# A hybrid attention layer on one core: how far ahead weight loads are issued, and where the summing steps of the output weights stand

## The chip, the cores and the metric

The kernel runs on one core of a Trainium2 chip. Its engines are TensorE (PE, matmuls), VectorE (DVE), ScalarE (ACT), GpSimd (POOL) and SyncE (SP, which here only issues DMA transfers). The metric is device time in microseconds; the profile gives the starts and durations of the instructions on each engine.

## The reference

One layer on 512 tokens and 16 meta tokens (528 positions) of width 2048, in fp32:

```python
hn = rmsnorm(h, pre_norm_g)
qa, ka, va, ga, qb, kb, vb, gb = split(hn @ w_in)     # widths 1024, 256, 256, then five of 1024
# mixer A: 8 query heads of 128 on 2 key/value heads, RMS-normed q and k, rotary
ya = softmax(rope(norm(qa)) @ rope(norm(ka)).T / sqrt(128)) @ va * silu(ga)
# mixer B: 8 heads, each with two score matrices on 64 of the 128 columns
a  = softmax(q1 @ k1.T / 8 + bias) - lam * softmax(q2 @ k2.T / 8 + bias)
yb = rmsnorm(a @ vb, sub_g) * (1 - lambda_init) * silu(gb)
y  = concat(ya, yb) @ w_out
out = h + rmsnorm(y, post_norm_g)                     # without the meta tokens
```

## The kernel before

**Precision and chunks.** Every fp32 operand of a matmul is split into a high and a low part, and a product is three matmuls (high by high, low by high, high by low). The weights of a projection come in chunks of 512 KB: a load into a tile `st` (L149, on SP's queue), the high part `wh` by ACT (L156), the low part `wl` by DVE (L157), then 24 or 48 matmuls for the eight 128-row pieces in it (`pd`). The pool `wp` has three buffers each of `st`, `wh` and `wl`. `todo` lists the chunks to come, `chunks` those whose load and split are written into the program; `fetch` keeps two beyond the one in hand. In this kernel a chunk's load and its two splits are thus always written together.

**Stage B (to about 490 us).** For each of 8 heads the projections of gate, value, key and query (two chunks each, `dense_T`) run while the attention of an earlier head is woven between their matmuls: scores `sc` (L61, psum), added bias and row maximum (`mx`, `p`, DVE L521), exponentials (`p`, `sm`, ACT L529), the reciprocal (DVE L531), the scaling of the first p by GpSimd (L534), the difference of the two p by DVE (L536), 32-by-32 transposes (`pt`, DVE), a turn through DRAM (`turn` out, L455; four pieces of `pl` and one of `pt` back, L461 and L462, all on SP's queue), the split of that into `ph` (ACT), `pl` (DVE) and `pm`, and p times v (`pv`). The query of the next head is split by L337 (`q`, four pieces, ACT) and L340 (`l`, four pieces, DVE).

**Sums of output weights.** The output product of the last stage uses 32 blocks `ws` of 512 KB in DRAM that are sums of blocks of `w_out` with each other. Each sum is one step: a transfer on SP's queue (L141: a copy `ws<-ws` of an earlier sum, or a load `ws<-in_w_o_dram`), and an adding DMA on GpSimd's queue (L809). `weigh(n)` takes n steps; of each it first issues the add that belongs to the step before, so that one load is always waiting for its add. It is called at three places of a head: two steps ahead of the gate, two after it, and one after the values.

**Stages A and C.** From about 490 to 745 us the 8 heads of mixer A follow (normalization and rotary of q and k: `qn`, `kn`; transposed queries split into `qh` and `qlA`; scores, `mxA`, p, turn and `pv` as above), between the projections of A and the 8 gates (`gt`, with a table load on ACT before and after the gate's own function). Then come the output products `po`, which load chunks of `ws` and `w_out` into `st` by the same `fetch`, and the end at 908 us.

**What sets the order.** PE's order and that of the loads written by `load()` (L141) are the program's. Tasks of attention are put between dense matmuls by `Lanes`: a virtual clock counts the matmuls' time, and a task sleeps for a lag from the table `LAG` (in us of that clock; `pB` and `pA` are the lags from the regrouping of p to p times v in mixers B and A). The order on ACT, DVE, GpSimd and of the other DMAs on SP is chosen when the program is built, by a scheduler that goes by priorities (the splits of weights have a raised one) and by its own idea of when operands are ready. Each engine and each queue works strictly in the order so set.

Of the kernel before, what the change touches and what calls it, by code (L numbers as in the profile page):

```python
# [10 lines left out]
F32 = mybir.dt.float32  # L11
# [3 lines left out]
ALU = mybir.AluOpType  # L15
AX = mybir.AxisListType

P = 128
# [11 lines left out]


LAG = dict(vals=3.5, bank=2.8, bankA=1.5, bankB=2.5, turnA=1.5, turnB=1.5, pvA=5.0, pvB=6.0, scB=3.0,
           pB=22.0, ss=6.0, qA=2.35, scA=5.1, pA=16.0, rope=10.2, head=3.85, fin=1.35, qn=1.4, norm=4.0, valsA=(10.0, 7.0),
           steps=(3.0, 2.5, 2.0, 2.0), stepsK=(2.5, 2.0, 1.5))

AHEAD = -60
# [70 lines left out]
def kernel(ctx: ExitStack, tc: tile.TileContext, xT, xn, xm, w_s, w_t, w_q, w_o,  # L107
                             gpre, gq, gk, lams, gsub, gpost, ident_d, cos_d, sin_d, dist_d, out):
    nc = tc.nc
# [6 lines left out]
    wp = ctx.enter_context(tc.tile_pool(name="wp", bufs=3))  # L116
# [22 lines left out]
    def load(out, in_):  # L139

        tc.keep_in_program_order(nc.sync.dma_start(out=out, in_=in_))  # L141


    def wload(src, n=1024, dma=nc.sync.dma_start, parts=1):
        st = wp.tile([P, 1024], F32, name="st", tag="st")
        ws = None
        for i in range(parts):
            c = slice(i * n // parts, (i + 1) * n // parts)
            dma(out=st[:, c], in_=src if parts == 1 else src[:, c])  # L149
            ws = wsplit(st, c, ws)  # L150
        return ws
# [43 lines left out]
    KEYS = [(0, HALF), (HALF, NT)]  # L195
    REAL = [(NM, NT)]
# [4 lines left out]
        mm(ps, wl, xh[k][:, n0:n1], start=False, stop=(k == KT - 1))  # L201


    todo, chunks = [], []

    def fetch(ahead=2):
        while todo and len(chunks) <= ahead:
            src = todo.pop(0)
            chunks.append(src() if callable(src) else wload(src))
        return chunks.pop(0)  # L210

    def dense_T(segs, pss=None, half=None):

        pss = pss or [pd.tile([P, 512], F32, name="pd", tag="pd") for _ in segs]
        for k0 in range(0, KT, 8):
            wh, wl = fetch()
            for k in range(k0, k0 + 8):
                c = slice((k - k0) * P, (k - k0 + 1) * P)
                for (n0, n1), ps in zip(segs, pss):
                    three(ps[:, :n1 - n0], wh[:, c], wl[:, c], k, n0, n1)  # L220
                    lanes.poll()
                if half and k == 8:
                    half()
        return pss
# [38 lines left out]
    for t in (TT, 0, 1, 2, 3):  # L263
        rows = P if t < TT else NM
        src = xn[t * P:(t + 1) * P, :] if t < TT else xm
        for j in range(2 if t < 2 else 4):

            tag, w = ("pl", "pt")[j % 2], 1024
# [73 lines left out]
    def keys_B(pss, after=nullcontext):  # L342
        kf = ap.tile([P, NT], F32, name="kf", tag="tT")
        halves(pss, kf)
        s1 = ap.tile([P, NT], F32R, name="s1", tag="s1")
        s2 = ap.tile([P, NT], F32R, name="s2", tag="s2")
        with after():
            hi(s1[L], kf[L])
            hi(s2[U], kf[U])
            lo(s1[U], kf[L], s1[L])  # L350
            lo(s2[L], kf[U], s2[U])
        return s1, s2
# [43 lines left out]
    def values(pss, lag=LAG["vals"]):  # L396

        vf = ap.tile([P, NT], F32, name="vf", tag="tT")
        halves(pss, vf)
        vh = ap.tile([P, TT, P], F32R, name="vh", tag="vh")  # L400
        vl = ap.tile([P, TT, P], F32R, name="vl", tag="vl")
        vm = ap.tile([96, P], F32R, name="vm", tag="vm")
        nc.vector.memset(vm.bitcast(F32), 0.0)

        def turn():
            yield from whole()
            tr = ptr.tile([P, 512], F32, name="tr", tag="tr")
            for c in range(TT):
                transpose(tr[:, c * P:(c + 1) * P], vf[:, NM + c * P:NM + (c + 1) * P], ident)
            tv = tr.rearrange("p (c d) -> p c d", d=P)  # L410
            hi(vh, tv)
            lo(vl, tv, vh)
            yield LAG["bank"]
            yield from whole()
            tr = ptr.tile([P, 512], F32, name="tr", tag="tr")
            transpose(tr[:NM, :P], vf[:, 0:NM], ident)
            hi(vm[0:NM], tr[0:NM, :P])
            hi(vm[64:64 + NM], tr[0:NM, :P])
            lo(vm[32:32 + NM], tr[0:NM, :P], vm[0:NM])

        return (vh, vl, vm), lanes.spawn(turn(), lag)

    def gate(pss, name):
        g = gp.tile([P, SEQ], F32, name=name, tag="g", bufs=4)
        nc.vector.tensor_tensor(out=g, in0=pss[0], in1=rB[:, NM:], op=ALU.mult)
        nc.scalar.activation(g, g, AF.Silu)
        return g
# [369 lines left out]
    steps, adds = [], []  # L797
# [4 lines left out]
        steps += [(S[2][i], S[1][i], block(p, 0, 1, i)) for i in range(4)]  # L802
        steps += [(S[3][i], block(p, 0, 0, i), block(p, 1, 0, i)) for i in range(4)]

    def weigh(n=1):
        for _ in range(n):
            if adds:
                dst, src = adds.pop(0)
                nc.gpsimd.dma_start(out=dst, in_=src, accum_op=ALU.add)  # L809
            if steps:  # L810
                dst, src, add = steps.pop(0)
                load(dst, src)
                adds.append((dst, add))

    def otile(name, n, dt=F32R):
        return xtile(name, n, dt)[:, NM:NT]
# [48 lines left out]
    def finish_head(h):  # L865
        lanes.finish(heads[h])
        lanes.finish(over[h])

    for h in range(NH):
        heads[h] = lanes.spawn(attention_B(h, qs, ks, *v), LAG["head"], heads[h - 1])  # L870
        if h == 2:
            tables()
        if h > 0:
            weigh(2)
            gB[h] = gate(dense_T(REAL), f"gB{h}")
        if h + 1 < NH:
            if h:
                weigh(2)
            pss = dense_T(KEYS)
            if h:  # L880
                finish_head(h - 1)
            v = values(pss)
            if h:
                weigh()
            ks = keys_B(dense_T(KEYS))
            qs = queries_B(h + 1, dense_T(REAL))
    weigh()
    def start_heads(grp, qn, q_task, k, v):
# [76 lines left out]
    def product(ops, pss, more=False, beside=None, done=None, ahead=2):  # L965


        def step(u, i, ws):
            for j in range(2):
                bh, bl = ops(i, j, u)  # L970
                c = slice(j * 512, (j + 1) * 512)
                wh, wl = ws[j] if isinstance(ws, list) else [w[:, c] for w in ws]
                mm(pss[u], bh, wh, start=(i + j == 0 and not more), stop=False,
                   skip_group_check=more)
                mm(pss[u], bl, wh, start=False, stop=False, skip_group_check=more)
                mm(pss[u], bh, wl, start=False, stop=(i + j == 4), skip_group_check=more)
                lanes.poll()

        for i in range(1 if done else 4):
            ws = fetch(ahead)  # L980
            for u in range(2):
                step(u, i, ws)
            if beside:
                beside(i)
        if done:
            last = [fetch(len(todo)) for _ in range(3)]
            for u in range(2):
                for i in range(3):
                    step(u, 1 + i, last[i])
                done(u, pss[u])  # L990
        return pss
# [259 lines left out]
```

## Time and profile before

| | us |
|---|---|
| median of 3 runs | 913.62 |
| lowest and highest | 912.55, 913.66 |
| the profiled execution, its own time | 910.12 |
| its span, from the first to the last instruction | 908.3 |
| mean granted TensorE clock | 0.984 of full speed |

The tables of the prediction come from this one execution. A row of a timeline has the start in us, the duration in us, the engine, the line of the kernel, the operation, output and inputs by their names, shapes, how many such instructions stand together (x4), and in brackets the engine's idle time ahead of the first of them with what ended it. `SPq` is the queue of SyncE; a row of it shows the issue of a DMA, not its transfer. In a row of the transfers' table stand what is moved, the count, the size of one and the median time from issue to landing. A row of a table by windows has the stretch, its length, then the busy time and the count of instructions of PE, PE's weight loads, DVE, ACT and POOL, then the granted clock, the share of the 16 DMA engines and GB/s.

### The profile page before, as it was taken

To read this page: it belongs to the slowest core of one execution; us is meant where nothing else is said; L and a number is where in the kernel's file an instruction comes from. 1 tells how busy PE (TensorE), PEld (TensorE's weight loads), DVE (VectorE), ACT (ScalarE), POOL (GpSimd) and SP (SyncE) were. 2 spreads that over 40 slices of the span, in tenths; PEclk is the share of its full clock that TensorE was granted. 3 is DMA by queue.
4 is the path that set the end of the run, shared out by engine and by line. 5 is a ranking of instruction groups with operands and counts; after the bars stand their busy time and mean duration, and the time that the engine had idled before them with its cause. 6 is when DMAs were issued, how large, how long until landed. Compare 5 with 4: busy or idle time off the path is not lost. (4 is left out here: it accounts for less than half of the span.)

```text
span 908.3 us, 14068 instructions
## 1 busy us (share of the span) xinstructions
PE 877.6 (97%) x5130; PEld 777.5 (86%) x5130; DVE 633.0 (70%) x1137; ACT 498.6 (55%) x844; POOL 126.7 (14%) x168
## 2 busy tenths in 40 slices
PE   9999999799989999999999999989989899999996
PEld 8999898798979989899898888978878788888884
DVE  6677785576846868575783485788664775876886
ACT  6564664445646456473754444566674565665561
POOL 0101112011111211111020021341211120000010
PEclk9999999899999999999999999999999899999998
DMA  9748759678595785968353334456566568889883
GB/s 342 260 152 238 196 180 264 169 227 218 158 287 131 225 255 157 291 171 254 115 180 93 105 92 153 136 156 180 169 167 187 179 197 306 289 284 305 294 257 150
DMA packets 80677, 185.49 MB, mean 204 GB/s; under 512 B 15136, under 2 KB 38560, under 8 KB 80224
## 3 DMA queue, kind: packets, MB, share of 16 engines
q1 hardware_dynamic: 75856, 167.81, 56.4%
q0 software_dynamic: 4608, 16.78, 10.7%
q8 instruction: 40, 0.66, 0.3%
q14 instruction: 29, 0.24, 0.1%
q10 hardware_dynamic: 144, 0.01, 0.0%
HBM read 158.34 MB, written 59.77 MB: 240 GB/s over the span
## 5 line engine op out<-in xcount | busy, mean ns | idle before, releaser
L61 PE MATMUL pd<-xh,wh 128*128 128x264 f32 (+1 forms) x992 | 328.6, 331 | 0.1
L61 PE MATMUL pd<-xl,wh 128*128 128x264 f32 (+1 forms) x992 | 325.7, 328 | 0.1
L61 PE MATMUL pd<-xh,wl 128*128 128x264 f32 (+1 forms) x992 | 324.6, 327 | 0.0
L156 ACT ACTIVATE wh<-st 128x1024 fp32r<-128x1024 f32 (+2 forms) x159 | 165.4, 1041 | 187.0 <-PE pd L61 95.4
L157 DVE TENSOR_TENSOR wl<-st,wh 128x1024 fp32r<-128x1024 f32 (+2 forms) x159 | 191.1, 1202 | 92.9 <-ACT wh L156 91.3
L61 PEld LDWEIGHTS pd<-xh,wl 128*128 128x128 f32 x992 | 188.3, 190 | 16.3 <-DVE wl L157 0.2
L61 PEld LDWEIGHTS pd<-xh,wh 128*128 128x128 f32 x992 | 188.8, 190 | 12.6 <-ACT wh L156 0.4
L61 PEld LDWEIGHTS pd<-xl,wh 128*128 128x128 f32 x992 | 188.9, 190 | 11.1 <-DVE xl L192 0.4
L529 ACT ACTIVATE p<-p,mx 128x528 f32<-128x528 f32 x64 | 47.1, 736 | 57.0 <-DVE mx L521 56.8
L448 DVE STREAM_TRANSPOSE pt<-p 128x512 f32<-128x512 f32 x64 | 45.2, 706 | 10.7 <-POOL p L629 9.9
L534 POOL TENSOR_SCALAR p<-p,sm 128x528 f32<-128x528 f32 x32 | 23.0, 718 | 208.9 <-DVE sm L531 208.7
L61 PE MATMUL pd<-wh,xh 128*128 128x512 f32 x128 | 50.4, 394 | 0.0
L61 PE MATMUL pd<-wh,xl 128*128 128x512 f32 x128 | 49.9, 390 | 0.0
L61 PE MATMUL pd<-wl,xh 128*128 128x512 f32 x128 | 49.9, 390 | 0.0
L521 DVE CUSTOM_DVE_ANT_0 p<-sc,dist 128x528 f32<-128x528 f32 x64 | 44.0, 688 | 6.5 <-PE sc L61 6.0
L627 ACT ACTIVATE p<-p,mxA 128x528 f32<-128x528 f32 x32 | 23.5, 735 | 40.1 <-DVE mxA L624 40.0
L340 DVE TENSOR_TENSOR pl<-pl,ph 128x1024 fp32r<-128x1024 f32 x32 | 40.4, 1261 | 5.7 <-ACT ph L337 5.2
L61 PE MATMUL sc<-s,q 128*128 128x264 f32 x128 | 35.6, 297 | 8.9 <-DVE mx L521 6.6
L809 POOL DMA_DIRECT2D ws<-in_w_o_dram x32 | 26.6, 841 | 121.9 <-DMA ws<-ws 54.2
L629 POOL TENSOR_SCALAR p<-p,smA 128x528 f32<-128x528 f32 x32 | 25.8, 806 | 122.1 <-DVE smA L628 118.4
L61 PE MATMUL pv<-ph,vh 128*128 128x256 f32 x128 | 37.2, 291 | 2.9 <-DMA st<-in_w_t_dram 2.9
L536 DVE SCALAR_TENSOR_TENSOR p<-p,c 128x528 f32<-128x528 f32 x32 | 24.5, 766 | 21.4 <-POOL p L534 21.2
(223 smaller groups left out, 1578.8 us busy)
## 6 DMA issues: line engine op xcount, KB each, us to landing
st<-in_w_t_dram SPq DMA_DIRECT2D x82, 512.0 KB, 5.5
turn<-pt SPq DMA_DIRECT2D x32, 544.0 KB, 3.0
ws<-in_w_o_dram POOLq DMA_DIRECT2D x32, 512.0 KB, 9.3
pl<-turn SPq DMA_DIRECT2D x128, 128.0 KB, 3.7
st<-ws SPq DMA_DIRECT2D x32, 512.0 KB, 4.5
st<-in_w_o_dram SPq DMA_DIRECT2D x22, 512.0 KB, 4.7
ws<-in_w_o_dram SPq DMA_DIRECT2D x16, 512.0 KB, 7.5
ws<-ws SPq DMA_DIRECT2D x16, 512.0 KB, 6.3
```

Of the source, the lines that this page charges most:

```text
L61: self._add(self.nc.tensor.matmul(out, lhsT, rhs, start=start, stop=stop, **kw), us)
L156: splits.append((nc.scalar.activation(wh[:, c], st[:, c], AF.Copy), nc.vector.tensor_tensor(out=wl[:, c], in0=st[:, c], in1=wh[:, c].bitca ...
L157: nc.vector.tensor_tensor(out=wl[:, c], in0=st[:, c], in1=wh[:, c].bitcast(F32), op=ALU.subtract)))
L340: nc.vector.tensor_tensor(out=dst, in0=src, in1=h.bitcast(F32), op=ALU.subtract)
L448: nc.vector.transpose(pt[:, :1024].rearrange("p (m c t q) -> p c m t q", m=4, c=TT, t=2)[:, :, :, j], p[:, NM:].rearrange("p (c m q) -> p ...
L521: maxima.append(nc.vector.tensor_tensor_reduce(out=two(p), in0=sc[:, :, :HALF], in1=two(dist[:, w0:w0 + NT]), scale=-0.125 / slope(h), sca ...
L529: nc.scalar.activation(p2[m], p2[m], AF.Exp, scale=-1.0, bias=mx[:, m:m + 1], accum_out=sm[:, m:m + 1])
L534: nc.gpsimd.tensor_scalar(out=p2[0], in0=p2[0], scalar1=sm[:, 0:1], scalar2=1.0, op0=ALU.mult, op1=ALU.mult)
L536: nc.vector.scalar_tensor_tensor(out=p2[0], in0=p2[1], scalar=c2, in1=p2[0], op0=ALU.mult, op1=ALU.add)
L627: nc.scalar.activation(p, p, AF.Exp, scale=-1.0, bias=mx, accum_out=sm)
L629: nc.gpsimd.tensor_scalar(out=p, in0=p, scalar1=sm, scalar2=1.0, op0=ALU.mult, op1=ALU.mult)
L809: nc.gpsimd.dma_start(out=dst, in_=src, accum_op=ALU.add)
```

## The change

The change adds no instruction and takes none away; it moves them. It has four parts.

1. A load and its splits are written apart. A new `bring` issues the load of a chunk; the splits are written when `fetch` moves the chunk from `landing` to `chunks`. `fetch` keeps two loads issued beyond the chunks it has split. Tiles are as many as before.
2. `weigh` takes one step, not n, and is called at five places of a head: ahead of the gate, in the middle of it, after it, after the values' projection and after the keys'. An add follows two loads behind, not one.
3. The lag `pA` goes from 16 to 13.5.
4. The last product, which fetches all that is left, counts `landing` too.

```diff
-           pB=22.0, ss=6.0, qA=2.35, scA=5.1, pA=16.0, rope=10.2, ...
+           pB=22.0, ss=6.0, qA=2.35, scA=5.1, pA=13.5, rope=10.2, ...
...
-    todo, chunks = [], []
+    todo, chunks, landing = [], [], []
+
+    def bring():
+        src = todo.pop(0)
+        if not callable(src):
+            st = wp.tile([P, 1024], F32, name="st", tag="st")
+            nc.sync.dma_start(out=st, in_=src)
+            src = lambda: wsplit(st)
+        landing.append(src)
 
     def fetch(ahead=2):
-        while todo and len(chunks) <= ahead:
-            src = todo.pop(0)
-            chunks.append(src() if callable(src) else wload(src))
+
+        while (todo or landing) and len(chunks) <= ahead:
+            if not landing:
+                bring()
+            chunks.append(landing.pop(0)())
+        while todo and len(landing) < 2 and not callable(todo[0]):
+            bring()
         return chunks.pop(0)
...
-    def weigh(n=1):
-        for _ in range(n):
-            if adds:
-                dst, src = adds.pop(0)
-                nc.gpsimd.dma_start(out=dst, in_=src, accum_op=ALU.add)
-            if steps:
-                dst, src, add = steps.pop(0)
-                load(dst, src)
-                adds.append((dst, add))
+    def weigh():
+
+        if len(adds) > (1 if steps else 0):
+            dst, src = adds.pop(0)
+            nc.gpsimd.dma_start(out=dst, in_=src, accum_op=ALU.add)
+        if steps:
+            dst, src, add = steps.pop(0)
+            load(dst, src)
+            adds.append((dst, add))
...
         if h > 0:
-            weigh(2)
-            gB[h] = gate(dense_T(REAL), f"gB{h}")
+            weigh()
+            gB[h] = gate(dense_T(REAL, half=weigh), f"gB{h}")
+            weigh()
         if h + 1 < NH:
-            if h:
-                weigh(2)
             pss = dense_T(KEYS)
             if h:
+                weigh()
                 finish_head(h - 1)
             v = values(pss)
+            ks = keys_B(dense_T(KEYS))
             if h:
                 weigh()
-            ks = keys_B(dense_T(KEYS))
             qs = queries_B(h + 1, dense_T(REAL))
...
-            last = [fetch(len(todo)) for _ in range(3)]
+            last = [fetch(len(todo) + len(landing)) for _ in range(3)]
```

What this does to the order shows at three places. In the changed kernel the lines behind L202 have numbers 12 higher, and the loads of weights stand at L210.

GpSimd's queue where the attention of head 2 begins (the adds to `ws`, the products `pm` of the head before, the scalings `p`), before:

```order
L478 TENSOR_SCALAR pm_1660<-pm_1660 32x256
L809 DMA ws010_568<-in_w_o_dram 128x1024
L478 TENSOR_SCALAR pm_1776<-pm_1776 32x256
L809 DMA ws011_569<-in_w_o_dram 128x1024
L809 DMA ws012_570<-in_w_o_dram 128x1024
L809 DMA ws013_571<-in_w_o_dram 128x1024
L809 DMA ws020_572<-in_w_o_dram 128x1024
L809 DMA ws021_573<-in_w_o_dram 128x1024
L534 TENSOR_SCALAR p_1886<-p_1886,sm_1880 128x528
L534 TENSOR_SCALAR p_1962<-p_1962,sm_1956 128x528
```

and with the change:

```order
L490 TENSOR_SCALAR pm_1661<-pm_1661 32x256
L821 DMA ws010_568<-in_w_o_dram 128x1024
L490 TENSOR_SCALAR pm_1779<-pm_1779 32x256
L821 DMA ws011_569<-in_w_o_dram 128x1024
L821 DMA ws012_570<-in_w_o_dram 128x1024
L821 DMA ws013_571<-in_w_o_dram 128x1024
L546 TENSOR_SCALAR p_1887<-p_1887,sm_1881 128x528
L821 DMA ws020_572<-in_w_o_dram 128x1024
L546 TENSOR_SCALAR p_1963<-p_1963,sm_1957 128x528
L546 TENSOR_SCALAR p_2056<-p_2056,sm_2050 128x528
```

The first scaling of the head stands behind four adds of this group, not six.

SP's queue in head 4, about the second turn of the head, with the 42nd load of `st` as the first row in both, before:

```order
L149 DMA st_2900<-in_w_t_dram 128x1024
L455 DMA turn_2758<-pt_2613 128x1088
L141 DMA ws033_579<-in_w_o_dram 128x1024
L141 DMA ws100_580<-in_w_o_dram 128x1024
L461 DMA pl_2760<-turn_2758 32x4x256 x4
L462 DMA pt_2613<-turn_2758 32x4x64
L149 DMA st_2964<-in_w_t_dram 128x1024
L149 DMA st_3012<-in_w_t_dram 128x1024
L141 DMA ws101_581<-in_w_o_dram 128x1024
L141 DMA ws102_582<-in_w_o_dram 128x1024
```

and with the change (numbers of tiles differ, since tiles are now made earlier):

```order
L210 DMA st_2799<-in_w_t_dram 128x1024
L467 DMA turn_2759<-pt_2614 128x1088
L141 DMA ws032_578<-in_w_o_dram 128x1024
L210 DMA st_2870<-in_w_t_dram 128x1024
L473 DMA pl_2761<-turn_2759 32x4x256 x4
L474 DMA pt_2614<-turn_2759 32x4x64
L210 DMA st_2907<-in_w_t_dram 128x1024
L141 DMA ws033_579<-in_w_o_dram 128x1024
L210 DMA st_2969<-in_w_t_dram 128x1024
```

The 43rd load stands ahead of the return of `pl`, not behind it, and behind one load of `ws`, not two.

ACT in head 5, where p of the head before is split and the queries of the next are, before:

```order
L156 ACTIVATE wh_3543<-st_3541 128x1024
L337 ACTIVATE q1_3524<-qf_3522 64x4x4x32
L337 ACTIVATE q2_3525<-qf_3522 64x4x4x32
L337 ACTIVATE q1_3524<-qf_3522 64x4x4x32
L337 ACTIVATE q2_3525<-qf_3522 64x4x4x32
L337 ACTIVATE ph_3556<-pl_3331 128x1024
L337 ACTIVATE pm_3557<-pt_3178 32x256
```

and with the change:

```order
L156 ACTIVATE wh_3542<-st_3454 128x1024
L349 ACTIVATE ph_3557<-pl_3332 128x1024
L349 ACTIVATE q1_3527<-qf_3525 64x4x4x32
L349 ACTIVATE q2_3528<-qf_3525 64x4x4x32
L349 ACTIVATE q1_3527<-qf_3525 64x4x4x32
L349 ACTIVATE q2_3528<-qf_3525 64x4x4x32
L349 ACTIVATE pm_3558<-pt_3179 32x256
```

The high part of p has gone ahead of the four pieces of the query; on DVE its low part `pl` has likewise gone ahead of the four `l`. The same holds in heads 4, 6 and 7.

More of the change, by code (lines that the diff above doesn't have):

```diff
@@ L32 @@
 LAG = dict(vals=3.5, bank=2.8, bankA=1.5, bankB=2.5, turnA=1.5, turnB=1.5, pvA=5.0, pvB=6.0, scB=3.0,
-           pB=22.0, ss=6.0, qA=2.35, scA=5.1, pA=16.0, rope=10.2, head=3.85, fin=1.35, qn=1.4, norm=4.0, valsA=(10.0, 7.0),
+           pB=22.0, ss=6.0, qA=2.35, scA=5.1, pA=13.5, rope=10.2, head=3.85, fin=1.35, qn=1.4, norm=4.0, valsA=(10.0, 7.0),
            steps=(3.0, 2.5, 2.0, 2.0), stepsK=(2.5, 2.0, 1.5))
```

## The prediction, made before the changed kernel had run

> **What bounds the kernel now.** I read the page first: the engines' busy time, the chain, then the transfers.
>
> ```profile
> span 908.3 us, 14068 instructions
> PE 877.6 (97%) x5130; PEld 777.5 (86%) x5130; DVE 633.0 (70%) x1137; ACT 498.6 (55%) x844; POOL 126.7 (14%) x168
> PE po L61 16%; PE pd L61 9%; PE pv L61 2%; PE sc L61 1%; DMA pl<-turn 0%; DMA oscr<-oA 0%; DVE y L1139 0%; PE tr L64 0%; ACT jko L1054 0%; DVE y L1057 0%; DVE y L1145 0%; DVE qlA L340 0%; ACT L627 0%; DVE pl L340 0%; DVE p L624 0%
> st<-in_w_t_dram SPq DMA_DIRECT2D x82, 512.0 KB, 5.5
> ```
>
> TensorE is busy for 97% of the span and the matmuls lead the chain. As the change takes away no matmul, it can win only what PE now spends waiting, or running slowly. So the second view is PE's timeline, of which I take the rows where it waited (the bracket gives the idle time ahead of the row and what ended it), two rows of undisturbed flow, and one matmul that the change will touch:
>
> ```profile
> 172.26 0.59 PE L61 MATMUL sc<-s,q 128*128 128x264 f32 x1 [5.89 <-DVE mx L521]
> 213.87 0.39 PE L61 MATMUL sc<-s,l 128*128 128x264 f32 x1 [0.46 <-DVE l L340]
> 270.57 0.39 PE L61 MATMUL sc<-s,q 128*128 128x264 f32 x1 [2.21 <-ACT q L337]
> 272.00 0.52 PE L61 MATMUL sc<-s,l 128*128 128x264 f32 x1 [1.04 <-DVE l L340]
> 326.37 0.39 PE L61 MATMUL pd<-xl,wh 128*128 128x512 f32 x1
> 326.59 0.39 PE L61 MATMUL pd<-xh,wl 128*128 128x512 f32 x1
> 327.13 0.39 PE L61 MATMUL sc<-s,l 128*128 128x264 f32 x1
> 611.73 0.39 PE L61 MATMUL sc<-kh,qh 128*128 128x264 f32 x1 [3.08 <-ACT qh L337]
> 680.46 0.39 PE L61 MATMUL sc<-kh,qh 128*128 128x264 f32 x1 [2.12 <-ACT qh L337]
> 708.65 0.39 PE L61 MATMUL pv<-ph,vh 128*128 128x256 f32 x1 [2.92 <-DMA st<-in_w_t_dram]
> 710.10 0.58 PE L61 MATMUL pv<-pl,vh 128*128 128x256 f32 x1 [0.94 <-DVE pl L340]
> ```
>
> Five places matter. I call them S1 (head 2, 172), S2 (head 4, 270 to 272), S3 (612), S4 (680) and S5 (709 to 710, which I count with both its rows). The third view, busy time by windows, shows that each costs more than its idle time; its last three columns are the granted clock, the DMA share and GB/s:
>
> ```profile
> 172.00:175.00 3.00, 2.74 (x12) 2.74 (x13) 3.00 (x6) 0.83 (x2) 0.00 (x0) 0.50 0.67 191
> 213.50:216.50 3.00, 2.63 (x13) 2.28 (x14) 2.91 (x4) 1.75 (x3) 2.09 (x3) 1.00 0.84 249
> 682.00:684.00 2.00, 2.00 (x9) 1.71 (x8) 0.88 (x3) 0.83 (x2) 0.07 (x1) 0.50 0.63 257
> 709.00:712.00 3.00, 2.06 (x9) 1.71 (x8) 2.94 (x4) 0.85 (x1) 1.25 (x1) 0.50 0.59 171
> ```
>
> After 5.89, 2.12 and 2.92 us of idleness the granted clock is 0.50; after 0.46 us it stays 1.00. Three microseconds at half the clock lose 1.5, so I price the slow stretch at 1.7 us, and at 2.6 for S5, where a second wait falls into it. A third part: in flow matmuls start 0.22 us apart (326.37, 326.59) though each is drawn 0.39 long, so a bracket leaves out some 0.2, which I take as 0.3 a place. Thus S1 costs 5.89 + 1.7 + 0.3 = 7.9, S2 2.21 + 1.04 + 1.7 + 0.3 = 5.3, S3 3.08 + 1.7 + 0.3 = 5.1, S4 2.12 + 1.7 + 0.3 = 4.1 and S5 2.92 + 0.94 + 2.6 + 0.3 = 6.8: 29.2 us together, of 908.3. That is the most that better order can win, short of the start and the tail.
>
> On the clock, the Trainium skill, page "TensorE: Matmul & The Clock Gate", table "Why this matters for your kernels", asks only that there be no idle gap over some 3 us, one idle window of which brings the half rate back. This trace disagrees: 2.12 us were enough at S4. By the rule the waits of some 1.2 us that I find below would never slow the clock; the fourth rival prices that.
>
> **S1: the output weights' steps.** GpSimd's queue is in order.
>
> ```profile
> 154.09 0.47 SPq L141 DMA_DIRECT2D ws<-ws  x1
> 167.35 0.81 POOL L809 DMA_DIRECT2D ws<-in_w_o_dram  x1 [8.72 <-DMA ws<-ws]
> 168.25 0.70 POOL L534 TENSOR_SCALAR p<-p,sm 128x528 f32<-128x528 f32 x1
> 161.00 0.17 DVE L531 RECIPROCAL sm<-sm 128x2 f32<-128x2 f32 x1 [0.90 <-ACT p L529]
> 168.99 0.77 DVE L536 SCALAR_TENSOR_TENSOR p<-p,c 128x528 f32<-128x528 f32 x1 [6.85 <-POOL p L534]
> ```
>
> The normalization p was ready to start when its reciprocal was done, at 161.2, but stood behind an adding transfer, and that behind its copy, issued at 154.09 and landed 13 us later. VectorE waited 6.85 us for p, and PE for what stood behind that on VectorE. In the changed order the adds ahead of this p end two steps earlier (ws013, not ws021), and their copies are no longer the fourth to sixth megabyte-moving copy in a row. ws012 and ws013 now follow the load whose buffer came free just before 154, so I take 154.1 for their issue. How long such a pair takes I bound from two other heads:
>
> ```profile
> 200.36 1.14 SPq L141 DMA_DIRECT2D ws<-in_w_o_dram  x2
> 213.80 0.81 POOL L809 DMA_DIRECT2D ws<-in_w_o_dram  x1 [12.03 <-DMA ws<-in_w_o_dram]
> 249.84 1.67 SPq L141 DMA_DIRECT2D ws<-in_w_o_dram  x2
> 258.59 0.83 POOL L809 DMA_DIRECT2D ws<-in_w_o_dram  x1 [0.79 <-DMA ws<-in_w_o_dram]
> ```
>
> The pair of 200.36 let its add go 13.4 us after issue, that of 249.84 after 8.75. With the shorter one p starts at 154.1 + 8.75 + 0.8 = 163.7 instead of 168.25; PE's wait of 5.9 shrinks by 4.6 to 1.3, or, as there are fewer copies at work, to nothing. With the longer, p starts at 168.3 and nothing is won. I take the short one, since the queue of copies ahead is halved, and 0.4 for what is left: **-7.5**; the other end is 0.
>
> **S2 and S5: loads ahead of other transfers.** Rows of SP's queue (the last is for later), of DVE and of ACT:
>
> ```profile
> 257.76 1.14 SPq L149 DMA_DIRECT2D st<-in_w_t_dram  x2
> 247.51 1.22 DVE L157 TENSOR_TENSOR wl<-st,wh 128x1024 fp32r<-128x1024 f32 x1
> 267.64 1.06 ACT L156 ACTIVATE wh<-st 128x1024 fp32r<-128x1024 f32 x1 [5.00 <-DMA st<-in_w_t_dram]
> 699.79 0.90 SPq L149 DMA_DIRECT2D st<-in_w_t_dram  x2
> 312.86 1.74 SPq L461 DMA_DIRECT2D pl<-turn  x4
> ```
>
> There are three st buffers, before and after, so no load can go out until the split three chunks back has read its buffer. In head 4 that split ended at 248.73 (247.51 + 1.22), yet the load went out at 257.76, behind the turn, two ws loads and the return of pl. In the new order it stands right behind the turn and one ws load: some 8 us earlier. Its split then waits for PE's buffers, not for a landing. ACT's q, which stood behind that split, comes some 5 us earlier; both rows of S2 go: **-5.3**. At S5 the same: the load of 699.79 had stood behind a turn, three ob loads and pl, and now goes out one turn earlier and, on ACT, ph goes ahead of the next wh. I leave 0.2: **-6.6**. What this costs: turn and pl return behind one more 512 KB load, 5.5 us by the page if they had to wait for all of it. p times v comes 22 us of PE work after the regrouping (pB), so this is covered, except where pl is wanted early: next part.
>
> **What the new order costs in heads 4 to 7 of B.** As pl's split (ph, pl) is now ahead of the queries' split on both engines:
>
> ```profile
> 323.73 2.58 ACT L337 ACTIVATE q<-qf 64x512 fp32r<-64x512 f32 x4
> 325.00 2.80 DVE L340 TENSOR_TENSOR l<-qf,q 64x512 fp32r<-64x512 f32 x4
> 327.83 1.23 DVE L340 TENSOR_TENSOR pl<-pl,ph 128x1024 fp32r<-128x1024 f32 x1
> 676.43 1.04 ACT L337 ACTIVATE ph<-pl 128x1024 fp32r<-128x1024 f32 x1
> ```
>
> The third of the four l ends at about 325.00 + 3/4 of 2.80 = 327.1, and the matmul that reads it started at 327.13: no slack. With pl's 1.23 us ahead of l, PE waits 1.2 us in each of four heads: **+4.8**. At best something hides them (0), at worst each brings the half clock too (4 x 2.9 = 11.6). Between 0.46 us idle (clock kept) and 2.12 (lost), 1.2 lies nearer to the first; I take one in four.
>
> **S3, S4 and the rest of stage A.**
>
> ```profile
> 611.78 0.68 DVE L340 TENSOR_TENSOR qlA<-tr,qh 128x512 fp32r<-128x512 f32 x1
> 677.80 1.28 ACT L627 ACT_TABLE_LOAD   x1
> 679.83 0.58 ACT L337 ACTIVATE qh<-tr 128x512 fp32r<-128x512 f32 x1
> ```
>
> At S3 qh no longer stands behind an exponential, but VectorE has other splits and sums to finish ahead of qlA in the new order as well, and PE's next matmul needs that one too, so I grant only **-0.6** of 5.1. At S4 two table loads of 1.28 us stood ahead of qh; in the new order both stand behind it, with ph, pm and p ahead: qh starts near 678.9 instead of 679.83, and I leave 1.3: **-2.8**. With the first p times v task of A coming four triples earlier (pA 13.5), the exponential, the table loads and ph change places on ACT at four more points of the stage; the queries' turn near 582 and 632 and two pv near 700 to 720 get waits of 0.45, 1.3, 1.5 and 1.0 by these durations: **+4.3**. Bounds: 0 if there is slack, 8 if none.
>
> **Free edits.** In the output products, loads go out two chunks earlier against the y and ts loads on SP, which so come up to two loads (11 us, of 5.5 each) later in the queue. PE's list has no wait worth a row behind 711, so I take nothing, with 2 us as the other bound. The last fetch takes the same three chunks. Bytes, instructions and splits are the same in number.
>
> **Sum.** -7.5 - 5.3 - 6.6 - 0.6 - 2.8 + 4.8 + 4.3 = -13.7. Eight new waits near 1.2 us, one in four with a slow stretch of 1.7: +3.4. Together -10.3. The profiled execution took 910.12 us with its span of 908.3; it would take 899.8. The median of the runs shown is 913.62, and 3.5 above this execution; I put the same 10.3 on it: **903.3 us**.
>
> **Rivals.** (1) All five go and the eight waits are hidden, as the loads' earlier landing moves everything on VectorE forward: -29.2 us, 884.4. For it: VectorE is 70% busy and could absorb 1.2 us; against it: l shows no slack at 327.1, and S3 has VectorE as its bound. Chance 0.13. (2) The pair lands as slowly as that of 200.36: S1 stays, -10.3 + 7.5 = -2.8, 910.8. Chance 0.13. (3) The change doesn't do what it says: with three buffers the load cannot run ahead. S2 and S5 stay: -10.3 + 11.9 = +1.6, 915.2. Against it stand 9 us between 248.73 and 257.76. Chance 0.05. (4) No slow stretch after any short wait: -13.7, 899.9; this is what the clock rule of the Trainium skill gives. Its opposite, one after each: -13.7 + 13.6 = -0.1, 913.5. Chances 0.15 and 0.05. (5) Slower: ph, now ahead of q on ACT in four heads, waits for pl's landing, and pl's return stands behind one more 512 KB load. Before, the four pieces went out by 314.6 (312.86 + 1.74) in head 5 and took 3.7 us by the page, so they were there at 318.3; ph's new place is at 323.73, a margin of 5.4 us. If pl comes later by more, q and l come later with it, and PE waits. At 7.8 us later each of the four heads loses 2.4 more, and the slow stretch is certain (1.7 instead of a quarter of it): 4 x (2.4 + 1.3) = 14.8, and 913.62 - 10.3 + 14.8 = 918.1. It decides from 6.7 us of delay on. Against it: one load takes 5.5 us by the page. Chance 0.07.
>
> **How the numbers follow.** The forecast has 0.42 by itself, 898 to 907; with rivals 2 and 4 and the bounds of stage A the range is **891 to 911.5**. It leaves out rival 1 at 884.4, most of 3, 4's second case and 5: a little over 0.2, but each of them shades off into the range. Under 0.2% (1.8 us) this kernel's runs can't be told apart. Faster: the forecast, 1, 2 (but for 0.02) and 4's first case: 0.81. Same: 4's second case, that part of 2, and 0.02 of 3: 0.09. Slower: 5 and the rest of 3: 0.10.
>
> **What would show it.** S1: the first p of head 2 on POOL before 165. S2: no DMA named ahead of wh near 267, and the load issued near 250. Heads 4 to 7: sc<-s,l with a bracket of 1.2 from DVE l. S5: no bracket from st. S3: still a bracket of 2 to 3 us. The prediction is wrong if waits of 1.2 us each bring 0.50 in the clock column, or if new brackets name pl<-turn.

## The result, and the profile after

| | median us | lowest, highest | runs |
|---|---|---|---|
| before | 913.09 | 904.29, 913.66 | 4 |
| changed | 900.28 | 897.44, 901.28 | 4 |

The ratio is 0.987, with a 95% interval of 0.9823 to 0.9917: 1.3% faster, between 0.8 and 1.8%. The profiled execution of the changed kernel took 901.28 us (before: 910.12), so of the two profiles the difference is 8.8. The kernel before spreads over 9 us from run to run, so its one profile is a point in that spread.

The page of the changed kernel, with the lines of span, busy time and loads that the prediction shows for the kernel before:

```profile
span 899.5 us, 14066 instructions
PE 870.3 (97%) x5130; PEld 769.9 (86%) x5130; DVE 631.4 (70%) x1137; ACT 497.9 (55%) x844; POOL 124.9 (14%) x168
st<-in_w_t_dram SPq DMA_DIRECT2D x82, 512.0 KB, 5.1
```

PE's busy time is 7.3 us less with the same matmuls, as fewer of them ran at half the clock (the mean granted clock is 0.997, before 0.984). PE's timeline, the larger waits:

```profile
170.68 0.39 PE L61 MATMUL sc<-s,q 128*128 128x264 f32 x1 [0.51 <-DVE mx L533]
261.84 0.39 PE L61 MATMUL sc<-s,l 128*128 128x264 f32 x1 [1.17 <-DVE l L352]
317.61 0.39 PE L61 MATMUL sc<-s,l 128*128 128x264 f32 x1 [1.17 <-DVE l L352]
372.49 0.39 PE L61 MATMUL sc<-s,l 128*128 128x264 f32 x1 [1.17 <-DVE l L352]
397.16 0.39 PE L61 MATMUL sc<-s,q 128*128 128x264 f32 x1 [0.90 <-DVE mx L533]
429.51 0.39 PE L61 MATMUL sc<-s,l 128*128 128x264 f32 x1 [1.16 <-DVE l L352]
604.46 0.36 PE L61 MATMUL sc<-kh,qh 128*128 128x264 f32 x1 [1.38 <-DVE mxA L636]
673.99 0.39 PE L61 MATMUL sc<-kh,qlA 128*128 128x264 f32 x1 [1.05 <-DVE qlA L352]
706.68 0.39 PE L61 MATMUL pv<-ph,vh 128*128 128x256 f32 x1 [0.52 <-ACT ph L349]
720.43 0.39 PE L61 MATMUL pv<-pl,vh 128*128 128x256 f32 x1 [1.48 <-DVE pl L352]
731.89 0.39 PE L61 MATMUL pv<-pl,vh 128*128 128x256 f32 x1 [1.43 <-DVE pl L352]
```

S1 and S2 are gone. The four waits on l are there, 1.17 us each. S3 has gone from 3.08 to 1.38 us, S4 from 2.12 to 1.05. S5 has gone from 2.92 to 0.52 us (706.68), but p times v now waits for its operands at several places. No wait is over 1.5 us, and the windows behind them, where the third column from the end is the granted clock, show full speed:

```profile
261.80:264.80 3.00, 2.96 (x14) 2.54 (x15) 1.96 (x5) 1.15 (x2) 0.25 (x1) 1.00 0.97 272
604.50:607.50 3.00, 2.37 (x15) 2.02 (x16) 3.00 (x9) 0.92 (x3) 0.80 (x1) 1.00 0.54 180
720.40:723.40 3.00, 2.97 (x18) 2.70 (x19) 2.60 (x6) 1.74 (x3) 0.00 (x0) 1.00 0.07 26
```

S5 was not a wait for a load, though the bracket of its row (708.65) names one. ScalarE's rows of the kernel before show what p times v waited for there:

```profile
705.88 0.73 ACT L627 ACTIVATE p<-p,mxA 128x528 f32<-128x528 f32 x1 [2.62 <-DVE mxA L624]
706.61 1.04 ACT L156 ACTIVATE wh<-st 128x1024 fp32r<-128x1024 f32 x1
707.56 1.04 ACT L337 ACTIVATE ph<-pl 128x1024 fp32r<-128x1024 f32 x1
```

ScalarE stood idle until the row maximum mxA was there, then made an exponential, then the high part of a chunk, and only then ph, which ended at 708.60. The load of that chunk, issued at 699.79, had landed at 705.58, before ScalarE got mxA. In weigh_alone and pA_alone, below, the same 2.92 us are put down to ph. In the changed kernel ph stands ahead of that chunk's split.

For comparisons below I use one more number from PE's timeline, the **loss** of a stage: the sum of the distances between the starts of consecutive matmuls, less what each takes in full flow (columns divided by 2253, in us; 0.227 for 512; a small transpose counts some 0.11). It holds waits and half speed together. Stage B counts up to 490 us, stage A from there to 750. Behind 750 it is about nil in every kernel but one (adds_long_behind, where it is some 1.4).

| kernel | loss in B | loss in A |
|---|---|---|
| before | 33.3 | 21.7 |
| changed | 28.5 | 17.8 |

Together 8.7, the difference of the spans (8.8).

### The profile page after: what moved, and what is told of

Same layout as the page of the kernel before. It is cut to its first block, busy times and chain, and to the rows that moved or that the text cites. A ratio compares the mean times of both kernels' runs of the same rounds, so it can differ in the third digit from the quotient of the medians.

```text
span 899.5 us, 14066 instructions
## 1 busy us (share of the span) xinstructions
PE 870.3 (97%) x5130; PEld 769.9 (86%) x5130; DVE 631.4 (70%) x1137; ACT 497.9 (55%) x844; POOL 124.9 (14%) x168
## 5 line engine op out<-in xcount | busy, mean ns | idle before, releaser
L61 PEld LDWEIGHTS pd<-xh,wh 128*128 128x128 f32 x992 | 186.8, 188 | 12.3 <-ACT wh L156 0.2
L61 PEld LDWEIGHTS pd<-xl,wh 128*128 128x128 f32 x992 | 187.0, 189 | 10.6
L639 ACT ACTIVATE p<-p,mxA 128x528 f32<-128x528 f32 x32 | 23.6, 737 | 46.2 <-DVE mxA L636 46.1
L61 PE MATMUL pv<-pl,vh 128*128 128x256 f32 x128 | 36.6, 286 | 4.4 <-DVE pl L352 4.4
L548 DVE SCALAR_TENSOR_TENSOR p<-p,c 128x528 f32<-128x528 f32 x32 | 24.5, 766 | 20.7 <-POOL p L546 20.5
```

Source lines behind the costliest of these rows:

```text
L61: self._add(self.nc.tensor.matmul(out, lhsT, rhs, start=start, stop=stop, **kw), us)
L548: nc.vector.scalar_tensor_tensor(out=p2[0], in0=p2[1], scalar=c2, in1=p2[0], op0=ALU.mult, op1=ALU.add)
L639: nc.scalar.activation(p, p, AF.Exp, scale=-1.0, bias=mx, accum_out=sm)
```

## The experiments

The first three parts of the change were each run alone (the fourth goes with the loads), and the whole without one; then the costs it was suspected to bring were taken away, doubled, or moved. The kernels of each of the three tables ran on one chip, with the kernel before in the same rounds. The kernel before had medians of 908.36, 912.06 and 909.34 there, so the ratios are to be compared, not the times across tables. A ratio sets a kernel's runs against those of the kernel before in its own rounds; it is not the quotient of these medians.

| first group | median us | ratio to before, 95% interval | loss in B | in A |
|---|---|---|---|---|
| steps alone (weigh_alone) | 900.8 | 0.9886 (0.9851 to 0.992) | 23.6 | 20.6 |
| loads alone (loads_alone) | 910.25 | 1.0012 (0.9984 to 1.0041) | 32.9 | 23.8 |
| pA alone (pA_alone) | 913.13 | 1.0031 (1.0002 to 1.0061) | 32.3 | 25.9 |
| steps and loads (without_pA) | 906.63 | 0.9954 (0.9928 to 0.9979) | 24.8 | 24.9 |

**The summing steps alone.** The edit, on the kernel before (the five places as in the change):

```diff
-    def weigh(n=1):
-        for _ in range(n):
-            if adds:
...
+    def weigh():
+
+        if len(adds) > (1 if steps else 0):
...
```

> The kernel before with only the new places of the summing steps (five single steps, adds two loads behind); loads and pA as before. In its order the first p of head 2 stands behind five adds (the changed kernel: four, before: six), the 43rd load is ahead of pl's return, ph is ahead of q in heads 4 to 7, and stage A has the order of before. Theory (each stall has its own cause, each part of the change its own places): S1 mostly gone, S2 gone, four new waits of 1.17 us, S3 to S5 as before; span 7 us below 908.3, some 901 to 904. Rival (the loads that run ahead do it all): same as before, S1 and S2 there.

PE's timeline and GpSimd's, where the scaling of p in head 6 is shown:

```profile
166.47 0.39 PE L61 MATMUL sc<-s,q 128*128 128x264 f32 x1 [0.30 <-DVE mx L521]
261.52 0.39 PE L61 MATMUL sc<-s,l 128*128 128x264 f32 x1 [1.17 <-DVE l L340]
601.99 0.55 PE L61 MATMUL sc<-kh,qh 128*128 128x264 f32 x1 [3.06 <-ACT qh L337]
698.26 0.58 PE L61 MATMUL pv<-ph,vh 128*128 128x256 f32 x1 [2.92 <-ACT ph L337]
376.93 0.71 POOL L534 TENSOR_SCALAR p<-p,sm 128x528 f32<-128x528 f32 x1 [5.85 <-DVE sm L531]
```

The theory by places holds and the rival falls: S1 and S2 are gone without any load running ahead, the waits on l are there, and S3 to S5 stand as before (S4 with 2.12 us). But the gain is more than the 7 us of the theory: the span is 897.5 against 908.3, and this one part gives a ratio as good as the whole change (0.9886 against 0.987). The last row tells something that I had not looked at: GpSimd stood idle for 5.85 us until the reciprocal of p was ready, so no add was in p's way.

A second cause of S1 shows in the kernel before, in a row of SP's timeline and in the waits of its queue (line, what was waited for, us in total, times, longest):

```profile
139.66 11.07 SPq L141 DMA_DIRECT2D ws<-ws  x2
```

```profile
SPq L141 <- DMA ws<-in_w_o_dram: 9.5, 1, 9.5
```

Once, for 9.5 us, inside that issue of 11.07, the whole queue stood behind a copy `ws<-ws` whose source was still being added to: the copy of ws020 copies ws010, and with double steps it came up before the add to ws010 had landed. That held up what came later in the queue, ws021 with it. In the changed kernel this wait is absent, and the first p of head 2 waits for its reciprocal, not for an add:

```profile
161.76 0.71 POOL L546 TENSOR_SCALAR p<-p,sm 128x528 f32<-128x528 f32 x1 [1.68 <-DVE sm L543]
```

**Loads alone.** The edit, on the kernel before (`bring` as in the change):

```diff
-        while todo and len(chunks) <= ahead:
-            src = todo.pop(0)
-            chunks.append(src() if callable(src) else wload(src))
+        while (todo or landing) and len(chunks) <= ahead:
+            if not landing:
+                bring()
+            chunks.append(landing.pop(0)())
+        while todo and len(landing) < 2 and not callable(todo[0]):
+            bring()
```

> The kernel before with only the loads running ahead of the splits; summing steps and pA as before. Theory: S2 and S5 gone (the brackets from st), S1 at most halved (five adds ahead of the first p of head 2), the four waits of 1.17 us there as well, S3 and S4 as before; span 6 to 9 us below 908.3. Rival (the loads that run ahead do it all): as the changed kernel, span near 899.5, S1 gone.

```profile
167.04 0.39 PE L61 MATMUL sc<-s,q 128*128 128x264 f32 x1 [0.85 <-DVE mx L533]
221.74 0.39 PE L61 MATMUL sc<-s,q 128*128 128x264 f32 x1 [1.48 <-DVE mx L533]
278.56 0.59 PE L61 MATMUL sc<-s,q 128*128 128x264 f32 x1 [2.33 <-DVE mx L533]
728.85 0.48 PE L61 MATMUL pv<-ph,vh 128*128 128x256 f32 x1 [3.67 <-ACT ph L349]
273.68 1.69 POOL L821 DMA_DIRECT2D ws<-in_w_o_dram  x2 [9.44 <-DMA ws<-in_w_o_dram]
275.45 0.70 POOL L546 TENSOR_SCALAR p<-p,sm 128x528 f32<-128x528 f32 x1
276.19 0.77 DVE L548 SCALAR_TENSOR_TENSOR p<-p,c 128x528 f32<-128x528 f32 x1 [6.13 <-POOL p L546]
```

Both theories miss the time: no gain at all, where I expected 6 to 9 us and the rival 9. The places came as I said (S2 gone, S5 gone at its place, S1 small, the waits on l there), but new waits ate it up. In stage B they are waits on mx, and the rows at 273 to 276 show their chain: it is S1 again in head 4. The first p stands behind two adds, those behind loads of ws still on their way, and VectorE waits 6.13 us. In stage A p times v at 729 waits 3.67 us for ph, which there stands on ScalarE behind an exponential, another split, a table load and a gate.

**pA alone.** The edit, on the kernel before:

```diff
-           pB=22.0, ss=6.0, qA=2.35, scA=5.1, pA=16.0, rope=10.2, ...
+           pB=22.0, ss=6.0, qA=2.35, scA=5.1, pA=13.5, rope=10.2, ...
```

> The kernel before with only pA 13.5. Theory: stage B as before with S1 and S2, no waits on l in heads 4 to 7; in stage A, S3 and S4 smaller and new waits on pl, the load of S5 still behind other transfers; span 2 to 5 us below 908.3. Rival (stage A only changes places of its waits): no change beyond 1.5 us.

```profile
608.32 0.36 PE L61 MATMUL sc<-kh,qh 128*128 128x264 f32 x1 [1.38 <-DVE mxA L624]
678.41 0.39 PE L61 MATMUL sc<-kh,qlA 128*128 128x264 f32 x1 [1.07 <-DVE qlA L340]
704.36 0.39 PE L61 MATMUL pv<-ph,vh 128*128 128x256 f32 x1 [2.92 <-ACT ph L337]
730.06 0.58 PE L61 MATMUL pv<-pl,vh 128*128 128x256 f32 x1 [1.92 <-DVE pl L340]
```

and the window behind the last of them (third column from the end: the clock):

```profile
730.00:733.00 3.00, 2.94 (x10) 2.65 (x11) 1.91 (x6) 0.40 (x1) 0.00 (x0) 0.50 0.06 24
```

S3 and S4 are as small as in the changed kernel, so the shorter lag, and nothing else, made them small. But the earlier p times v now waits longer for its operands, and the clock falls behind the last of them. Stage A loses 4 us more than before: the time is no better, 0.3% worse. My theory's gain is not there. The rival's bound of 1.5 us is passed by the profile (span 911.5, 3.2 more) but not excluded by the interval of the ratio, which is 0.2 to 5.5 us.

**Steps and loads, without pA.** The edit, on the changed kernel:

```diff
-           pB=22.0, ss=6.0, qA=2.35, scA=5.1, pA=13.5, rope=10.2, ...
+           pB=22.0, ss=6.0, qA=2.35, scA=5.1, pA=16.0, rope=10.2, ...
```

> The changed kernel with pA back at 16. Theory: stage B as in the changed kernel; in stage A S5 gone but S3 and S4 back with their slow clock (5.1 and 4.1 us by the prediction), the pl waits near 660, 707, 720 and 731 (0.8, 1.3, 1.5, 1.9) gone: 3 us above to 3 us below 899.5. Rival (pA is what won stage A): 4 us or more above 899.5.

```profile
603.12 0.59 PE L61 MATMUL sc<-kh,qh 128*128 128x264 f32 x1 [3.07 <-ACT qh L349]
672.56 0.39 PE L61 MATMUL sc<-kh,qh 128*128 128x264 f32 x1 [2.14 <-ACT qh L349]
721.76 0.58 PE L61 MATMUL pv<-ph,vh 128*128 128x256 f32 x1 [4.00 <-ACT ph L349]
```

S3 and S4 are back, and p times v at 722 waits 4 us. The rival's "4 us or more above" is nearer than mine by the medians (0.9954 against 0.987); the profile's span of 902.8 is 3.3 above. So in stage A the loads without pA lose (23.8 and 24.9 against 21.7), pA without the loads loses (25.9), and only both together win (17.8). Each is one profile, and two profiles of the changed kernel, below, differ by some 2 us in a stage. Over all of them the order holds: 17.8 to 20.0 in the five profiles with both and nothing moved in the adds, 20.6 to 22.9 in the four with neither. That is a win of some 2 us, not of 4.

| second group | median us | ratio to before, 95% interval | loss in B | in A |
|---|---|---|---|---|
| the changed kernel again (changed_again) | 898.76 | 0.9882 (0.9845 to 0.9919) | 26.3 | 19.9 |
| the same, queries' splits first (query_first) | 899.38 | 0.9876 (0.9837 to 0.9915) | 25.7 | 20.0 |
| steps alone, queries' splits first (weigh_query_first) | 897.13 | 0.9859 (0.9825 to 0.9893) | 20.7 | 21.1 |
| the changed kernel, longer waits on l (wait_longer) | 906.15 | 0.9939 (0.9909 to 0.9969) | 31.7 | 20.0 |

**The changed kernel again.**

> The changed kernel once more, on the same chip and in the same rounds as the next three, since the steps taken alone (900.8 for the summing steps) came out as fast as the whole. If the whole is worth more than the summing steps alone, it is below 900; if the loads and pA add nothing, 899 to 902, ratio 0.985 to 0.992; if they take something away on top, 902 to 904. Stage B loses some 28 us against full flow and stage A some 18 in its one profile so far; the theory now is that stage B repeats only within 3 us, as its waits hang on when transfers land.

0.9882, the same as the steps alone within the intervals, so the loads and pA together add nothing that can be measured to them. (By the median alone, 898.76 is just below the 900 of "worth more"; but the kernel before differs between the two groups as well, so I go by the ratio.) Two profiles of one kernel differ by 2 us in each stage.

**The waits on l taken away.** The edit, in the split of p, once on the changed kernel and once on the steps alone (`lastq` holds the last two instructions of the queries' splits):

```diff
-            hi(ph, pt)
-            hi(pm[0:32], pf)
-        lo(pl, pt, ph)
+            with tc.issue_after(lastq[0].ins):
+                hi(ph, pt)
+                hi(pm[0:32], pf)
+        with tc.issue_after(lastq[1].ins):
+            lo(pl, pt, ph)
```

> The changed kernel with the splits of p (ph, pl, pm) put behind the queries' splits in stage B, by two constraints of order; nothing else moves but one memset on VectorE. Theory (the four waits of 1.17 us are pl's split ahead of l, and nothing hides them): the four brackets on l go, 4 x 1.33 = 5.3 us less than the changed kernel in the same rounds, 0.6%. Rival (the later pl becomes the wait of p times v, or mx comes later behind it): less than 2 us gained.

> The summing steps alone, with the queries' splits first. Theory (steps do stage B, the order of the splits is a cost of its own): 5.3 us below the steps alone, 895.5; S3 to S5 stay. Rival (stage B then waits elsewhere): 899 to 901, as the steps alone.

The four waits on l are gone in both, so their cause is shown. What they were worth is not the same: on top of the steps alone the loss in B falls by 2.9 us (by about 3 in a second profile), and the ratio to 0.9859, an interval that overlaps that of the steps alone. On top of the changed kernel it falls by 0.6 and the ratio not at all: there waits on mx stand in their stead.

```profile
327.00 0.39 PE L61 MATMUL sc<-s,q 128*128 128x264 f32 x1 [1.19 <-DVE mx L537]
339.89 0.39 PE L61 MATMUL sc<-s,q 128*128 128x264 f32 x1 [0.88 <-DVE mx L537]
396.00 0.39 PE L61 MATMUL sc<-s,q 128*128 128x264 f32 x1 [0.89 <-DVE mx L537]
```

Both are below the 5.3 that the theory gave; the rival has it for the changed kernel.

Where the wait at 327 comes from show GpSimd's and VectorE's rows of query_first, and the scaling of the same p in weigh_query_first:

```profile
321.89 0.84 POOL L825 DMA_DIRECT2D ws<-in_w_o_dram  x1 [6.88 <-DMA ws<-ws]
324.74 0.77 DVE L552 SCALAR_TENSOR_TENSOR p<-p,c 128x528 f32<-128x528 f32 x1 [4.44 <-POOL p L550]
320.39 0.71 POOL L538 TENSOR_SCALAR p<-p,sm 128x528 f32<-128x528 f32 x1 [4.02 <-DVE sm L535]
```

With the loads ahead, the first p of head 5 stands behind two adds, the first of which waited 6.88 us for its copy, as at S1, and VectorE waits 4.44 us for p. With the steps alone the same p waits only for its reciprocal, and no wait on mx follows. VectorE has the same four reciprocals of 0.84 us ahead of a later mx in both kernels, so they are not what makes the difference.

**The waits on l made longer.** Edit:

```diff
         lo(pl, pt, ph)
+        if gate_of is None:
+            with tc.high_priority(-rank[0]):
+                nc.vector.tensor_scalar(out=pl, in0=pl.bitcast(F32), scalar1=1.0, scalar2=None,
+                                        op0=ALU.mult)
```

> The changed kernel with one more pass of VectorE over pl (times 1.0, in place) behind its split in stage B; in heads 4 to 7 it stands ahead of l, so the waits of 1.17 us grow by its length, 0.6 to 1.2, to 1.8 to 2.4. Theory (the clock falls between 1.5 and 2.1 us of idleness): where the wait comes above some 2 us the granted clock of the 3 us behind it is 0.50 and the place costs 1.5 more on top of its idle time. Rival (it takes some 3 us of idleness): clock 1.00 behind all four, and each place costs only its idle time.

```profile
320.54 0.39 PE L61 MATMUL sc<-s,l 128*128 128x264 f32 x1 [1.87 <-DVE l L352]
375.99 0.39 PE L61 MATMUL sc<-s,l 128*128 128x264 f32 x1 [1.87 <-DVE l L352]
```

and the windows behind these two:

```profile
320.50:323.50 3.00, 2.96 (x14) 2.54 (x15) 1.82 (x4) 1.08 (x2) 0.00 (x0) 1.00 0.85 289
376.00:379.00 3.00, 3.00 (x11) 2.50 (x12) 1.79 (x4) 0.94 (x1) 0.43 (x1) 0.74 0.85 272
```

The four waits grew to 1.77 us (265) and 1.87 (320, 376, 433). Of the three equal ones one (376) brought the clock down and the two others did not. So neither theory is borne out as it stands: the length of one wait alone does not decide it here. The loss in B is 5.4 us above that of changed_again, and only 2.7 of it are the longer waits; the rest holds the slow stretch and, among others, a wait on mx of 1.71 us at 169.

| third group | median us | ratio to before, 95% interval | loss in B | in A |
|---|---|---|---|---|
| query_first, adds four loads behind (adds_long_behind) | 913.95 | 1.0064 (1.0037 to 1.0091) | 44.8 | 19.3 |
| loads ahead from stage A on, queries' splits first (split_by_stage) | 895.09 | 0.984 (0.9807 to 0.9873) | 21.4 | 19.9 |
| weigh_query_first again (weigh_query_again) | 898.15 | 0.9874 (0.9845 to 0.9902) | about 20.5 | about 22.9 |

**Adds far behind.** Edit (with three more calls of `weigh` at the end):

```diff
-        if len(adds) > (1 if steps else 0):
+        if len(adds) > (3 if steps else 0):
             dst, src = adds.pop(0)
-            nc.gpsimd.dma_start(out=dst, in_=src, accum_op=ALU.add)
+            with tc.issue_after(scaled[-1].ins):
+                nc.gpsimd.dma_start(out=dst, in_=src, accum_op=ALU.add)
```

> The kernel query_first (the changed kernel, queries' splits first) with the adds four loads behind instead of two, each put behind the last scaling of p on GpSimd by a constraint of order; so the first p of a head never stands behind an add whose copy has just gone out. Theory (with loads ahead, the copies land later, the first p of a head waits in GpSimd's queue behind an add, and mx behind it on VectorE): in every head p waits for its reciprocal, not for an add; the brackets on mx near 327, 340, 391 and 396 go, stage B loses 21 instead of 25.7 us, 4 to 5 us below query_first. Rival (mx is late there because VectorE's own order is full, four reciprocals of 0.84 us ahead of it): the brackets stay, within 1.5 us of query_first.

A miss in the time by 19 us (894.5 was the theory's, from 4 to 5 us below query_first), though the waits on mx behaved as the theory says: those near 327 to 396 are gone. (PE now stands still right ahead of them, which gives VectorE time, so by itself this would not show that the adds had made them.) PE waits for q instead, as at S2, in five heads, behind a split that waits for its load. The timeline, and then SP's waits, which name the reason:

```profile
323.17 1.06 ACT L156 ACTIVATE wh<-st 128x1024 fp32r<-128x1024 f32 x1 [4.66 <-DMA st<-in_w_t_dram]
326.10 0.39 PE L61 MATMUL sc<-s,q 128*128 128x264 f32 x1 [2.56 <-ACT q L349]
387.12 0.39 PE L61 MATMUL sc<-s,q 128*128 128x264 f32 x1 [3.38 <-ACT q L349]
```

```profile
SPq L141 <- DMA ws<-in_w_o_dram: 41.4, 11, 9.0
```

Eleven times, 41.4 us in all, a copy of a sum stood in SP's queue until the add to its source had landed, and the loads of weights stood behind it. In query_first there is no such wait. So here an add that came too early held up GpSimd, and adds that came too late held up SP.

**Loads ahead from stage A on.** Edit: on query_first; the flag is set behind the last step of stage B:

```diff
-        while todo and len(landing) < 2 and not callable(todo[0]):
+        while todo and far[0] and len(landing) < 2 and not callable(todo[0]):
...
     weigh()
+    far[0] = True
```

> The changed kernel, but the loads run ahead only from stage A on, and queries' splits first in stage B: stage B as in weigh_query_first (20.7 us lost there), stage A as in the changed kernel (17.8 and 19.9 lost in its two profiles, against 21.1). Theory (the parts act by stage and do not depend on each other across stages): 1 to 3 us below weigh_query_first. Rival (stage A's gain depends on what stage B left in the queues): as weigh_query_first or slower.

> weigh_query_first once more, as the measure for the two others on this chip: 896 to 899, some 1.4% below the kernel before.

The fastest of all, 895.09: 3.1 below weigh_query_first in the same rounds, the top of what was expected (the intervals of the two ratios overlap). Its profile loses 21.4 in B and 19.9 in A, so the theory holds and the rival falls.

This also says why the whole change is no better than its steps. The loads ahead cost stage B some 1 to 5 us: with queries first 25.7 against 20.7, without 24.8 to 28.5 (three profiles with steps and loads) against 23.6. Together with pA they win some 2 in stage A. The two come near to cancelling.

One part of the change was not run by itself, since it does nothing: built with adds one load behind, not two, all engines have the same instructions in the same order. So it is the scheduler, and not the place in the program, that sets where an add stands, as long as no constraint ties it down.

## Why the prediction was right, and where it was not

The time was forecast at 903.3 in 891 to 911.5, and came out at 900.28; against the profile's own time 899.8 was forecast and 901.28 found. The sign and the size are right, the size in part by luck. The median was had by putting 10.3 on 913.62, and the kernel before has medians of 908 to 913 in the four groups of runs; and rival 4's 899.9 is nearer to 900.28 than the forecast. By its steps:

- **S1, -7.5.** Right in place and near in size: the loss from 150 to 175 us fell from 7.8 to 1.3. The mechanism was named in half. The add waited for a slow copy, yes; but the copy was late also because SP's queue had stood 9.5 us behind a copy of an unfinished sum, a wait that I had not seen in the issue of 11.07 us.
- **S2, -5.3, put down to the loads.** It went, but weigh_alone shows that the single steps do it too; I had given to one part what either part brings.
- **l, +4.8.** Right in place, cause and length: four waits of 1.17 us, shown by query_first to come from pl's split ahead of l. They lose 5.3 together, but taking them away gained only 2.9 in stage B with the steps alone and 0.6 in the changed kernel.
- **Loads ahead cost the other transfers nothing.** This is the step that failed. I looked at the turn and pl, not at the ws transfers and the adds behind them on GpSimd. In loads_alone an add waited 9.44 us for its load, VectorE 6.13 for p behind it, and stage B lost by such waits about what S1 and S2 gave (32.9 against 33.3).
- **S3, -0.6, and S4, -2.8.** S3 was mis-sized: with its clock it cost 5.1 and now costs 2.3 (1.38 + 0.63 idle and 0.2 to 0.3). S4 is right. Both come from pA, as pA_alone shows.
- **S5, -6.6, and the new waits of stage A, +4.3.** S5 went, but its main cause was named wrongly: ph stood on ScalarE behind an exponential that waited for mxA and behind a split whose load had already landed, so an earlier load by itself could not have won it. What the prediction names second, ph ahead of the next wh, is what the changed kernel shows. It holds in every kernel with the loads ahead and in none without. The new waits cost nearly twice what I took: in the profile of the changed kernel those from 627 to 732, S4's left out, lose 8.0 together.
- **Slow clock, +3.4.** Mis-sized: none of the waits of up to 1.48 us brought it in that profile. The fourth rival, which takes this from the rule of the Trainium skill (page "TensorE: Matmul & The Clock Gate", table "Why this matters for your kernels"), had that part right for this profile. Against the rule stand pA_alone (0.82 and then 1.92 us, clock 0.50) and the second profile of the changed kernel, at the end. That second profile, with its slow stretches, loses 2.1 us more in stage A, so part of the miss is the luck of the first.

The errors cancel in large part: no slow clock (-3.4) and S3 (-2.2) against stage A's waits (+3.7), the waits on mx that I had not foreseen (4.0 from 285 to 453) and S1 (+1.0). They add up to +3.1; the profile came out 1.5 above the forecast, so some of the difference is not traced. That the sum came out is therefore no proof of its parts; the runs with single parts are what bears the explanation.

What stays open: how much slower the copies and the loads of ws land when loads run ahead was not measured apart from their place in SP's queue, so whether place or shared bandwidth makes the adds late isn't settled.

## What to carry to other kernels

A transfer moved forward in an in-order queue pushes all others back: follow those to whoever waits for them, on every engine, before you call the move free. Run the parts of a change alone: here one part gave the whole gain, one brought nothing alone, one lost, and only together, and only in one stage, did these two win anything. In a chain of dependent sums look at both queues: an add placed too early holds up the queue that it is in, and one placed too late holds up the copies that wait for its result. A bracket names what ended last by the profile; check on the engine that makes the operand whether it really waited for that.

## What was not expected of the hardware

Equal waits of PE do not always bring the clock down, and the same kernel differs in it from run to run. The same pair of waits near 602 us in the changed kernel (1.38 or 1.39 us, then 0.63) left the clock at 1.00 in its first profile and not in its second, of which this is the window:

```profile
603.50:606.50 3.00, 3.00 (x13) 2.72 (x14) 3.00 (x12) 0.83 (x2) 1.05 (x2) 0.56 0.21 81
```

The first profile is the exception. Nearly the same pair (1.39 to 1.55 us, then 0.63) was followed by a clock of 0.60 to 0.71 in query_first, wait_longer, split_by_stage and adds_long_behind too, and so was the pair near 730 (0.42 us, then 1.44 some 2 us later) in all five (0.50 to 0.63). A single wait of 1.48 us near 720 left the clock at 1.00 in all six. In wait_longer 1.87 us did it at one place of three. The kernel before, with five longer waits, varied by 9 to 14 us between runs (904.96 to 918.61 in the second group), the one with the single steps and the queries first by 2 to 3 (896.72 to 898.79, and 896.6 to 899.5 in the third group).
